# Seven block products in place of eight in the down projection of a decoder layer

## The chip, the cores and the metric

The kernel runs on one core of one Trainium2 chip. The metric is the device time of one execution in microseconds (us). A core has a matrix engine (PE; PEld is its loading of the stationary operand), a vector engine (DVE), an activation engine (ACT), a GpSimd engine (POOL) and a queue (SP) from which all loads and stores of this part are issued. Each engine works through its own instructions in order and waits where an operand is not there yet.

## The reference

One decoder layer on 512 tokens of width 1024: a token mixer with a residual, then a gated convolutional feed-forward part with a residual, then a final RMSNorm. The change touches the last matrix product of the feed-forward part, the residual beside it and the final norm:

```python
D_MODEL = 1024; SEQ = 512; FFN_DIM = 2816
def conv_ffn(h, w_up, conv_w, conv_b, w_down):
    up = h @ w_up
    ... # causal depthwise convolution of width 3, plus conv_b
    gate, val = jnp.split(up, 2, axis=-1)
    return (jax.nn.silu(gate) * val) @ w_down
...
    x = x + conv_ffn(h, w_up[l], conv_w[l], conv_b[l], w_down[l])
return rmsnorm(x, norm_final)
```

The down projection is thus a product of 512 tokens by 2816 (k) with 2816 by 1024 columns, in float32.

## The kernel before

Every float32 operand of a matrix product is split into a high part that the matrix engine takes whole (`whi`, `gh`, `hTh`) and the low rest (`wlo`, `gl`, `hTl`), and each product is three matmuls (`mm3`, `mm3m`): high by high, high by low, low by high. A matmul takes 128 of k and 128 stationary columns and streams 512 moving columns.

The order of all work is written out by hand. `units` is a list of pieces of PE work, each with the weight chunk that it needs; `run` goes through it, and for each unit it first has the chunks of the next ones loaded (SP), split (`Chunk.split`: ACT copies the high part, DVE subtracts it to get the low one), then emits what was put into `plan` with `before` or into `later`, and then the unit's matmuls. The list `early` says which chunks are split some units ahead. High and low pieces of weights have four buffers each (`whi`, `wlo`), so ACT may write a new one only when PE is through with the one that was there four pieces earlier.

The feed-forward part has two stages. In the up stage 11 steps of c each make 256 of the 2816 hidden values: four units of 24 matmuls (gate and value, two tiles of 128 each), whose results pass through the convolution (`conv`: one ACT instruction, two of DVE), silu and the product gate times value; the product is split into `gh` and `gl`, which stay in SBUF for all 22 tiles of k. In the down stage the tokens are the stationary operand and the weights move: for each half of 512 columns there are six chunks of up to four k tiles, and four accumulators in PSUM, one for each tile of 128 tokens (`down_unit`). After the first half the sum is added to the residual `x1` (which stays in SBUF), squared for the norm, and multiplied by the gain of the final norm. The last chunk of the second half goes token tile by token tile, so that the first three tiles are finished while PE works on the next; the last tile is done in two pieces of 256 columns. `finish` takes the reciprocal root on POOL, scales one half on ACT and the other on DVE, and stores them.

## Time and profile before

| what | value |
|---|---|
| median of 3 runs | 839.66 us (839.02 to 839.73) |
| profiled execution: time | 839.8 us |
| profiled execution: span from first to last instruction | 838.0 us |
| PE busy | 815.6 us (97% of the span) |
| DVE, ACT, POOL busy | 474.1, 354.5, 164.5 us |
| granted clock of TensorE, mean | 0.991 of full |

The span is what the trace covers; the time of an execution also has 1.8 us around it. A busy share is the time in which an engine had an instruction under way. The matmuls of PE overlap: one that lasts 0.39 us in the trace starts 0.227 us after the one ahead of it, so the pitch from start to start is the cost of one in a row of them.

### The profile page before, as it was taken

Reading aid. Unit: us, or ns where it says so; the run is one execution under the profiler, and the core shown is the slowest. Engines: PE = TensorE matmul, PEld = TensorE weight load, DVE = VectorE, ACT = ScalarE, POOL = GpSimd, SP = SyncE. Lnnn points to the kernel's source line nnn. Section 1 sums busy time; section 2 is a strip of 40 time slices with the busy share of each in tenths; the row PEclk is TensorE's granted clock in tenths of the full one; section 3 lists DMA queues with packets and bytes.
Section 4 is the critical chain, followed back from the end, with each engine's and each line's share of the span. In section 5 each row is a group of like instructions: output and inputs, shape, how many; then the busy total and the mean of one; then the engine's idle time right before and its main releaser. Section 6 shows DMA issues by size and latency. Waiting matters only on the chain.

```text
span 838.0 us, 10521 instructions
## 1 busy us (share of the span) xinstructions
PE 815.6 (97%) x4085; PEld 675.9 (81%) x4085; DVE 474.1 (57%) x921; ACT 354.5 (42%) x665; POOL 164.5 (20%) x217
## 2 busy tenths in 40 slices
PE   8999899997999999999999999999999999999996
PEld 7978768775787888888878998888888888888885
DVE  7998387484645637263655456555655555422313
ACT  6446455434435555352444344444444443313212
POOL 6199652441200100023520000000000000002002
PEclk9999989998999999999999999999999999999999
DMA  9332031121322113232261313333233323412402
GB/s 241 102 104 97 1 100 52 51 79 46 78 68 90 52 51 102 79 101 72 101 236 65 101 52 101 101 101 100 101 101 100 102 76 101 153 61 89 151 0 101
DMA packets 68277, 76.60 MB, mean 91 GB/s; under 512 B 8160, under 2 KB 55556, under 8 KB 68228
## 3 DMA queue, kind: packets, MB, share of 16 engines
q1 hardware_dynamic: 67972, 75.89, 28.2%
q8 instruction: 32, 0.52, 0.3%
q0 software_dynamic: 256, 0.05, 0.1%
q14 instruction: 17, 0.14, 0.1%
HBM read 73.81 MB, written 2.12 MB: 91 GB/s over the span
## 4 chain that ended last, share of the span: by engine, by line
PE 80%; POOL 8%; DVE 6%; ACT 2%; issue 2%; DMA 2%; SPq 0%; POOLq 0%; DVEq 0%; ACTq 0%
PE up L171 10%; PE up L172 10%; PE up L173 10%; PE mm L171 9%; PE mm L173 9%; PE mm L172 9%; PE acc L178 6%; PE acc L179 6%; PE acc L177 6%; POOL esc L279 1%; POOL vt L279 1%; POOL t L279 1%; PE sc L898 1%; DMA raw<-in_w_in_dram 1%; PE o L722 1%
## 5 line engine op out<-in xcount | busy, mean ns | idle before, releaser
L92 DVE TENSOR_TENSOR wlo<-raw,whi 128x1024 fp32r<-128x1024 f32 (+1 forms) x126 | 150.0, 1200 | 136.0 <-ACT whi L66 135.8
L66 ACT ACTIVATE whi<-raw 128x1024 fp32r<-128x1024 f32 (+1 forms) x126 | 127.3, 1023 | 58.3 <-PE acc L179 56.2
L171 PE MATMUL up<-hTh,whi 128*128 128x512 f32 (+1 forms) x384 | 142.7, 372 | 0.0
L172 PE MATMUL up<-hTl,whi 128*128 128x512 f32 (+1 forms) x384 | 142.6, 371 | 0.0
L173 PE MATMUL up<-hTh,wlo 128*128 128x512 f32 (+1 forms) x384 | 142.6, 371 | 0.0
L171 PE MATMUL mm<-hTh,whi 128*128 128x512 f32 (+1 forms) x336 | 133.9, 399 | 2.7 <-ACT whi L66 2.7
L173 PE MATMUL mm<-hTh,wlo 128*128 128x512 f32 (+1 forms) x336 | 131.3, 391 | 1.6 <-DVE wlo L92 1.6
L172 PE MATMUL mm<-hTl,whi 128*128 128x512 f32 (+1 forms) x336 | 130.9, 390 | 0.0
L275 DVE SCALAR_TENSOR_TENSOR cc<-up,cpar,cc 128x511 f32<-128x511 f32 x88 | 65.9, 749 | 97.3 <-ACT cc L1110 95.7
L173 PEld LDWEIGHTS up<-hTh,wlo 128*128 128x128 f32 x384 | 72.4, 188 | 12.6
L171 PEld LDWEIGHTS up<-hTh,whi 128*128 128x128 f32 x384 | 72.4, 188 | 12.5
L172 PEld LDWEIGHTS up<-hTl,whi 128*128 128x128 f32 x384 | 72.4, 188 | 12.4
L171 PEld LDWEIGHTS mm<-hTh,whi 128*128 128x128 f32 x336 | 64.3, 191 | 17.9 <-ACT whi L66 3.1
L173 PEld LDWEIGHTS mm<-hTh,wlo 128*128 128x128 f32 x336 | 64.2, 191 | 15.2 <-DVE wlo L92 2.0
L172 PEld LDWEIGHTS mm<-hTl,whi 128*128 128x128 f32 x336 | 64.2, 191 | 11.9
L177 PE MATMUL acc<-whi,gh 128*128 128x512 f32 x172 | 66.9, 389 | 0.0
L178 PE MATMUL acc<-wlo,gh 128*128 128x512 f32 x172 | 66.9, 389 | 0.0
L179 PE MATMUL acc<-whi,gl 128*128 128x512 f32 x172 | 66.9, 389 | 0.0
L279 POOL TENSOR_TENSOR x<-x,gfin 128x512 f32<-128x512 f32 x4 | 5.2, 1289 | 296.8 <-ACT acc L1049 296.8
L1110 ACT ACTIVATE cc<-up,cpar 128x512 f32<-128x512 f32 x44 | 34.3, 779 | 61.2 <-PE up L173 60.4
L992 ACT ACTIVATE th<-mm 128x512 f32<-128x512 f32 x24 | 14.3, 594 | 75.2 <-PE mm L173 75.2
L66 ACT ACTIVATE gh<-cc 128x512 fp32r<-128x512 f32 x22 | 13.9, 632 | 59.4 <-DVE cc L279 59.4
(298 smaller groups left out, 1266.1 us busy)
## 6 DMA issues: line engine op xcount, KB each, us to landing
raw<-in_w_up_dram SPq DMA_DIRECT2D x22, 1024.0 KB, 5.1
raw<-in_w_in_dram SPq DMA_DIRECT2D x18, 1024.0 KB, 5.1
raw<-in_w_down_dram SPq DMA_DIRECT2D x10, 1024.0 KB, 5.0
x<-in_x_dram SPq DMA_DIRECT2D x8, 512.0 KB, 6.6
raw<-in_w_in_dram SPq DMA_DIRECT2D x8, 512.0 KB, 5.3
raw<-in_w_out_dram SPq DMA_DIRECT2D x4, 1024.0 KB, 5.1
raw<-in_w_branch_a_dram SPq DMA_DIRECT2D x4, 512.0 KB, 6.0
raw<-in_w_branch_c_dram SPq DMA_DIRECT2D x2, 1024.0 KB, 5.0
```

What stands on the lines that cost most here:

```text
L66: S.activation(o, i, AF.Copy)
L92: (lo_eng or V).tensor_tensor(view(lo), r, view(hi).bitcast(F32), op=ALU.subtract)
L171: PE.matmul(ps, wh, xh, start=first, stop=False)
L172: PE.matmul(ps, wh, xl, start=False, stop=False)
L173: PE.matmul(ps, wl, xh, start=False, stop=last)
L177: PE.matmul(ps, xh, wh, start=first, stop=False)
L178: PE.matmul(ps, xh, wl, start=False, stop=False)
L179: PE.matmul(ps, xl, wh, start=False, stop=last)
L275: emit(lambda: V.scalar_tensor_tensor(o, a, s, b, op0=op0, op1=op1))
L279: emit(lambda: (eng or V).tensor_tensor(o, a, b, op=op))
L992: S.activation(t, ps, AF.Tanh, scale=0.5)
L1110: S.activation(dst, ps, AF.Identity, bias=cpar[:, 3, f:f + 1], scale=cpar[:, 2, f:f + 1])
```

## The change

The down projection is cut into halves of tokens, of k tiles and of columns, and these blocks are combined by a scheme of seven products (Strassen's, in Winograd's form): p1 to p7, each of 256 tokens by 1408 of k by 512 columns. Tokens and weights are first combined by sums and differences of blocks. For the weights, `Sum` loads one block at a time and, where `plus` names another, adds that one's raw block on DVE before the split: p5 is its own block plus that of p1, p6 adds p5's sum, p4 adds p6's sum, and p7 adds p3's block; p1, p2 and p3 use their block as it is. For the tokens, `sums` makes the combinations when a step of the up stage is done, and `late` splits the ones that have to wait for room.

The hidden values of each step c are the two halves of k (a = 0 and 1 of step c), so the scheme's k runs over 11 tiles, in groups of two (and one of one). There are two sweeps over k: the first accumulates p1, p5, p6 and p4 (eight banks of PSUM), the second p2, p7 and p3. Each pair of a group and a product is one unit: 12 matmuls, or 6 in the group of one (k0 = 10), which stands last in the first sweep and first in the second. `ends` puts the seven results together. The residual is written to DRAM in the up stage (`park`) and read back into the space of `hTh` when the up stage is over (`down_loads`); loads use six half-size buffers. The final norm is one instruction for each half row, after the last product.

```diff
+    class Sum:
+        def __init__(self, k0, nk, col, row):
+            self.k0, self.nk, self.col, self.row = k0, nk, col, row
...
+        def split(self, i, hi_eng=None, lo_eng=None):
+            r = self.raw
+            if self.plus is not None:
+                V.tensor_tensor(r, r, self.plus.raw, op=ADD)
+            hi, lo = (piece([128, 2, 512], n)[:, 0:self.nk, :] for n in ("whi", "wlo"))
+            copy_act(hi, r)
+            V.tensor_tensor(lo, r, hi.bitcast(F32), op=SUB)
+            self.p[0] = (hi, lo)
...
-                load_to(ci + 3)
+                load_to(ci + (6 if isinstance(c, Sum) else 3))
...
-            gh[f], gl[f] = slot([128, T], F32R, name="gh"), slot([128, T], F32R, name="gl")
-            copy_act(gh[f], v)
-            later.append(lambda: tt(gl[f], v, gh[f][:, :].bitcast(F32), SUB))
+            if a:
+                later.append(lambda: sums(c))
...
+    def sums(c):
...
+        v = cc[0][:, 2:4, :]
+        a11, a12, a21, a22 = (v[:, j, t * 256:t * 256 + 256] for t in range(2) for j in range(2))
+        s5 = s6 = a21
+        tt(R[c - c % 2, 4][:, Q1 if c % 2 else Q0], a11, a21, SUB)
+        tt(s5, a21, a22, SUB)
+        parts((c, 1), v[:, 0, :])
+        tt(s6, s5, a11, SUB)
+        two = lambda t: t.rearrange("p (j n) -> p j n", j=2)
+        if c < FULL:
+            parts((c, 2), v[:, :, Q1], two)
+        else:
+            R[c, 2] = store(F32)
+            copy_act(two(R[c, 2]), v[:, :, Q1])
+        R[c, 3] = store(F32)
+        copy_act(R[c, 3][:, Q0], a12)
+        tt(R[c, 3][:, Q1], a12, s6, ADD)
+
+    def late(c, i):
+        o = Q0 if (c, i) == (NP - 1, 4) else slice(0, T)
+        parts((c, i), R.pop((c, i))[:, o], lambda t: t[:, o])
...
+    def park():
+        for t in range(NT):
+            SY.dma_start(xd[t * 128:(t + 1) * 128, :], x1[t // 2][:, t % 2, :])
...
+    def down_loads():
+        SY.dma_start(x2[0], xd[:, :].rearrange("(t p) n -> p t n", p=128))
         SY.dma_start(gfin[0], norm_final[None, :].to_broadcast([128, DM]))
...
+    def down_unit(chunk, kind, k0, n, first, last):
         def fn():
...
+            for t in range(2):
+                if first:
+                    PS[kind, t] = bank(BANK[kind], name=kind)
+                for k in range(n):
+                    xh, xl = (v[:, t * 128:t * 128 + 128] for v in tok(k0 + k, kind))
+                    mm3m(PS[kind, t], xh, xl, chunk.get(k), first and k == 0,
+                         last and k == n - 1)
+                if last:
+                    ends(kind, t)
...
+    def ends(kind, t):
+        ps = PS[kind, t]
+        if kind == "p1":
+            es[t] = slot([128, 512], name="e")
+            copy_act(es[t], ps)
+            add_to(t, 0, ps)
+        elif kind == "p6":
+            tt(es[t], es[t], ps, ADD)
+        elif kind == "p4":
+            e, p5 = es[t], PS["p5", t]
+            add_to(2 + t, 0, e)
+            add_to(2 + t, 0, ps)
+            tt(e, p5, e, SUB)
+            later.append(lambda: (add_to(t, 1, e), add_to(2 + t, 1, e)))
+        elif kind == "p2":
+            add_to(t, 0, ps)
+            square(t, 0, ps)
+            part(t, 0)
+        elif kind == "p7":
+            add_to(2 + t, 0, ps)
+            add_to(2 + t, 1, ps, SUB)
+            square(2 + t, 0, ps)
+            square(2 + t, 1, ps)
+            part(2 + t, 0)
+            finish(2 + t)
+        elif kind == "p3":
+            add_to(t, 1, ps)
+            square(t, 1, ps)
+            finish(t)
...
     def finish(t):
+        ms = fss[:, 8 + t:9 + t]
+        part(t, 1)
         G.tensor_tensor(ms, ms, mhalf, op=ALU.pow)
...
+        for half in range(2):
+            o = slice(half * 512, half * 512 + 512)
+            stt(xv(t, half), xv(t, half), ms, gfin[0][:, o], MUL, MUL)
+            SY.dma_start(out[0, t * 128:(t + 1) * 128, o], xv(t, half))
...
+    SWEEPS = ((("p1", 0, 0, None), ("p5", 1, 0, "p1"), ("p6", 1, 1, "p5"), ("p4", 0, 1, "p6")),
+              (("p2", 0, 1, None), ("p7", 1, 0, "p3"), ("p3", 1, 1, None)))
+    GROUPS = [(c, min(2, NP - c)) for c in range(0, NP, 2)]
...
+    for i, (u, ch) in enumerate(sums_):
+        for d in (2, 3):
+            if i + d < len(sums_):
+                early.setdefault(u, []).append((sums_[i + d][1], 1))
...
+    before(u_up + 3, park)
+    before(u_down, down_begin)
+    before(u_down + 2, down_loads)
```

How the order of instructions moves is seen best on DVE, at three places. The first is the middle of the down stage. Before, DVE has only the subtractions that make the low parts of the weights:

```order
L92 TENSOR_TENSOR wlo_6023<-raw_5926,whi_6022 128x1024 [waits DMAHW1_49,Activation_49]
L92 TENSOR_TENSOR wlo_6027<-raw_5926,whi_6026 128x1024 [waits Activation_49]
L92 TENSOR_TENSOR wlo_6081<-raw_5969,whi_6080 128x1024 [waits DMAHW2_49,Activation_49]
L92 TENSOR_TENSOR wlo_6085<-raw_5969,whi_6084 128x1024 [waits Activation_49]
L92 TENSOR_TENSOR wlo_6139<-raw_6030,whi_6138 128x1024 [waits DMAHW4_49,Activation_49]
```

In the changed kernel this is one group of the first sweep (k0 = 4), from the split of p1 to that of p4; L187 is the sum of two raw blocks, L190 the subtraction for the low part, and `op` the low part of a late token combination:

```order
L190 TENSOR_TENSOR wlo_6098<-raw_5912,whi_6097 128x1024 [waits DMAHW2_49,Activation_49]
L308 TENSOR_TENSOR op_6103<-op_5283,op_6102 128x512 [waits Activation_49]
L187 TENSOR_TENSOR raw_5912<-raw_5912 128x1024 [waits DMAHW3_49]
L190 TENSOR_TENSOR wlo_6120<-raw_5912,whi_6119 128x1024 [waits Activation_49]
L187 TENSOR_TENSOR big_5989<-big_5989,raw_5912 128x1024 [waits DMAHW4_49]
L190 TENSOR_TENSOR wlo_6138<-big_5989,whi_6137 128x1024 [waits Activation_49]
L187 TENSOR_TENSOR big_5989<-big_5989 128x1024 [waits DMAHW7_49]
L190 TENSOR_TENSOR wlo_6156<-big_5989,whi_6155 128x1024 [waits Activation_49]
```

Three sums have come in, and each stands right ahead of the subtraction of the same block, which waits for ACT (the high part of that sum).

The second place is where the first sweep ends and the second begins; before, the nearest thing is the end of the first half of columns:

```order
L92 TENSOR_TENSOR wlo_6197<-raw_6088,whi_6196 128x1024 [waits DMAHW5_49,Activation_49]
L279 TENSOR_TENSOR x10_3896<-x10_3896,acc_5933 128x512 [waits PE_49]
L275 SCALAR_TENSOR_TENSOR fss_152<-fss_152,epsv_78 128x1 [waits Activation_49]
L279 TENSOR_TENSOR x10_3896<-x10_3896,acc_5934 128x512 [waits PE_49]
L275 SCALAR_TENSOR_TENSOR fss_152<-fss_152,epsv_78 128x1 [waits Activation_49]
```

In the changed kernel `x2` is the residual, `e` a copy of p1's result, and p4 to p6 are accumulators; the rows run from the subtraction for p3 (k0 = 10) to the sum for p7 of the next group (k0 = 0):

```order
L190 TENSOR_TENSOR wlo_6439<-raw_5912,whi_6438 128x512 [waits Activation_49]
L308 TENSOR_TENSOR x2_5988<-x2_5988,e_6396 128x512 [waits DVE_49]
L308 TENSOR_TENSOR x2_5988<-x2_5988,p4_6065 128x512 [waits DVE_49,PE_49]
L308 TENSOR_TENSOR e_6396<-p5_6023,e_6396 128x512
L308 TENSOR_TENSOR x2_5988<-x2_5988,e_6402 128x512
L308 TENSOR_TENSOR x2_5988<-x2_5988,p4_6072 128x512 [waits DVE_49,PE_49]
L308 TENSOR_TENSOR e_6402<-p5_6030,e_6402 128x512
L190 TENSOR_TENSOR wlo_6456<-raw_5912,whi_6455 128x1024 [waits DMAHW7_49,Activation_49]
L308 TENSOR_TENSOR x2_5988<-x2_5988,e_6396 128x512 x2
L308 TENSOR_TENSOR x2_5988<-x2_5988,e_6402 128x512 [waits DVE_49]
L308 TENSOR_TENSOR x2_5988<-x2_5988,e_6402 128x512
L187 TENSOR_TENSOR big_5989<-big_5989 128x1024 [waits DMAHW1_49,DMAHW0_49]
```

The additions that combine the products stand between the splits of the next weights.

The third place is the end of the program. Before:

```order
L275 SCALAR_TENSOR_TENSOR fss_152<-fss_152 128x1 [waits Activation_49]
L279 TENSOR_TENSOR x11_3897<-x11_3897,fin_6533 128x256 [waits PE_49]
L279 TENSOR_TENSOR cc_4381<-x11_3897,gfin_5971 128x256 [waits DVE_49]
L279 TENSOR_TENSOR x11_3897<-x11_3897,fin_6534 128x256 [waits PE_49]
L269 TENSOR_SCALAR cc_4381<-cc_4381,fss_152 128x512 [waits Pool_49]
L279 TENSOR_TENSOR cc_4381<-x11_3897,gfin_5971 128x256 [waits DVE_49]
L275 SCALAR_TENSOR_TENSOR fss_152<-fss_152 128x1 [waits Activation_49]
L275 SCALAR_TENSOR_TENSOR fss_152<-fss_152 128x1 [waits DVE_49,Activation_49]
L269 TENSOR_SCALAR cc_4381<-cc_4381,fss_152 128x512 [waits Pool_49]
```

In the changed kernel, from the second addition of p7's second token tile on:

```order
L308 TENSOR_TENSOR x2_5988<-x2_5988,p7_6486 128x512
L304 SCALAR_TENSOR_TENSOR fss_152<-fss_152,epsv_78 128x1 [waits Activation_49]
L304 SCALAR_TENSOR_TENSOR fss_152<-fss_152 128x1 [waits DVE_49,Activation_49]
L304 SCALAR_TENSOR_TENSOR x2_5988<-x2_5988,fss_152,big_5989 128x512 [waits Pool_49]
L304 SCALAR_TENSOR_TENSOR x2_5988<-x2_5988,fss_152,big_5989 128x512
L308 TENSOR_TENSOR x2_5988<-x2_5988,p3_6503 128x512 [waits PE_49]
L304 SCALAR_TENSOR_TENSOR fss_152<-fss_152 128x1 [waits Activation_49]
L304 SCALAR_TENSOR_TENSOR x2_5988<-x2_5988,fss_152,big_5989 128x512 [waits Pool_49]
L304 SCALAR_TENSOR_TENSOR x2_5988<-x2_5988,fss_152,big_5989 128x512 [waits DVE_49]
L308 TENSOR_TENSOR x2_5988<-x2_5988,p3_6507 128x512 [waits PE_49]
L304 SCALAR_TENSOR_TENSOR fss_152<-fss_152 128x1 [waits Activation_49]
L304 SCALAR_TENSOR_TENSOR x2_5988<-x2_5988,fss_152,big_5989 128x512 [waits Pool_49]
```

For each token tile DVE now goes through the whole chain from the addition over ACT and POOL to the scaling before it takes the next one.

## Rows read from the trace of the kernel before

**Rows 1.** The page's busy times (share of the span) and instructions by engine.
```profile
PE 815.6 (97%) x4085; PEld 675.9 (81%) x4085; DVE 474.1 (57%) x921; ACT 354.5 (42%) x665; POOL 164.5 (20%) x217
```

**Rows 2.** Busy time by engine of the up and down stages; columns in the first line.
```profile
core 0: us, PE busy (x) PEld busy (x) DVE busy (x) ACT busy (x) POOL busy (x), PEclk, DMA share, GB/s
475.00:711.00 236.00, 236.00 (x1117) 198.65 (x1116) 139.11 (x177) 102.09 (x135) 0.00 (x0) 1.00 0.30 96
711.00:831.00 120.00, 120.00 (x542) 99.80 (x540) 38.57 (x46) 29.88 (x42) 9.56 (x9) 1.00 0.25 86
```

**Rows 3.** Timeline of PE, first and last matmul of the down stage: start, duration.
```profile
711.13 0.39 PE L177 MATMUL acc<-whi,gh 128*128 128x512 f32 x1
...
830.85 0.28 PE L179 MATMUL fin<-whi,gl 128*128 128x256 f32 x1
```

**Rows 4.** Groups of the down stage, 711 to 838 us: busy, mean ns of one | idle before.
```profile
L177 PE MATMUL acc<-whi,gh 128*128 128x512 f32 x172 | 66.9, 389 | 0.0
...
L92 DVE TENSOR_TENSOR wlo<-raw,whi 128x1024 fp32r<-128x1024 f32 x21 | 25.6, 1235 | 54.9 <-ACT whi L66 54.9
...
L279 DVE TENSOR_TENSOR x<-x,acc 128x512 f32<-128x512 f32 x8 | 5.5, 687 | 20.8 <-PE acc L179 20.8
...
L269 DVE TENSOR_SCALAR cc<-cc,fss 128x512 f32<-128x512 f32 x4 | 1.9, 481 | 0.7 <-POOL fss L1214 0.7
```

**Rows 5.** Timelines of DVE and ACT: start, duration, idle before.
```profile
604.80 1.22 DVE L92 TENSOR_TENSOR wlo<-raw,whi 128x1024 fp32r<-128x1024 f32 x1
605.93 0.68 DVE L279 TENSOR_TENSOR gl<-cc,gh 128x512 fp32r<-128x512 f32 x1
606.53 0.69 DVE L279 TENSOR_TENSOR cc<-cc 128x512 f32<-128x512 f32 x1
...
712.15 1.54 DVE L275 SCALAR_TENSOR_TENSOR cc<-up,cpar,cc 128x511 f32<-128x511 f32 x2 [3.18 <-ACT cc L1110]
...
738.53 1.06 ACT L66 ACTIVATE whi<-raw 128x1024 fp32r<-128x1024 f32 x1 [4.38 <-PE acc L179]
...
739.63 1.23 DVE L92 TENSOR_TENSOR wlo<-raw,whi 128x1024 fp32r<-128x1024 f32 x1 [4.21 <-ACT whi L66]
```

**Rows 6.** DMA issues of 560 to 838 us: count, KB each, median us to landing.
```profile
raw<-in_w_down_dram SPq DMA_DIRECT2D x10, 1024.0 KB, 5.0
raw<-in_w_down_dram SPq DMA_DIRECT2D x2, 512.0 KB, 3.3
```

**Rows 7.** Timeline of PE after a long idle stretch in the mixer.
```profile
201.81 1.11 PE L737 MATMUL pt<-ident,pj 128*128 128x128 f32 x4 [5.36 <-ACT pj L66]
...
206.56 0.63 PE L171 MATMUL mm<-hTh,whi 128*128 128x512 f32 x1
206.99 0.63 PE L172 MATMUL mm<-hTl,whi 128*128 128x512 f32 x1
...
207.83 0.40 PE L171 MATMUL mm<-hTh,whi 128*128 128x512 f32 x1
```

**Rows 8.** Busy time and granted clock (PEclk) of two stretches of the mixer, columns as in rows 2.
```profile
56.00:60.00 4.00, 2.99 (x25) 2.62 (x25) 3.96 (x6) 3.86 (x8) 4.00 (x7) 1.00 0.40 136
201.00:207.00 6.00, 5.19 (x15) 4.22 (x16) 4.61 (x12) 2.28 (x4) 0.00 (x0) 0.50 0.00 0
```

**Rows 9.** Timelines of the norm's steps: one token tile at mid-stage, and the last ones.
```profile
771.17 0.69 DVE L279 TENSOR_TENSOR x<-x,acc 128x512 f32<-128x512 f32 x1 [1.08 <-PE acc L179]
...
771.90 0.60 ACT L1049 ACTIVATE acc<-x 128x512 f32<-128x512 f32 x1 [2.00 <-DVE x L279]
...
772.65 0.16 DVE L275 SCALAR_TENSOR_TENSOR fss<-fss,epsv 128x1 f32<-128x1 f32 x1 [0.79 <-ACT acc L1049]
...
832.73 0.55 POOL L1214 TENSOR_TENSOR fss<-fss,mhalf 128x1 f32<-128x1 f32 x1 [2.05 <-DVE fss L275]
...
833.31 0.72 ACT L68 ACTIVATE x<-x,fss 128x512 f32<-128x512 f32 x1 [1.18 <-POOL fss L1214]
...
834.49 0.38 SPq L1222 DMA_DIRECT2D out_dram<-cc  x1
```

More of the change, by code (lines that the diff above doesn't have):

```diff
@@ L167, in krows, with block, load, get @@
         return c
+    class Sum:
+        def __init__(self, k0, nk, col, row):
+            self.k0, self.nk, self.col, self.row = k0, nk, col, row
+            self.src = w_down[0].rearrange("(k h p) n -> p k h n", h=2, p=128)
+            self.defs, self.p, self.own, self.plus = [1], {}, False, None
+        def block(self, col, row):
+            return self.src[:, self.k0:self.k0 + self.nk, row, col * 512:col * 512 + 512]
+        def load(self):
+            self.raw = raw_tile(self.nk)
+            SY.dma_start(self.raw, self.block(self.col, self.row))
+        def split(self, i, hi_eng=None, lo_eng=None):
[6 more added lines that the diff above has]
+            self.p[0] = (hi, lo)
+        def get(self, k):
+            return tuple(t[:, k, :] for t in self.p[0])
     def mm3(ps, w, xh, xl, first, last):
@@ L212, in load_to @@
             while state["loaded"] < min(n, len(order)):
+                if isinstance(order[state["loaded"]], Sum) and rn[0] >= 4 and not RB:
+                    return
                 order[state["loaded"]].load()
@@ L1112, in conv @@
         stt(dst[:, 2:T], ps[:, 0:T - 2], cpar[:, 0, f:f + 1], dst[:, 2:T], MUL, ADD)
-    gh, gl, cc = {}, {}, []
+    cc = []
     fps = {}
@@ L1210, in hybrid_block, with down_begin @@
-    parts, rest = [], []
+    gfin, x2, RS, RB, RW, rn = [], [], [], [], [], [0]
+    xd = dr.tile([T, DM], F32, tag="xd", bufs=1, name="xd")
+    def park():
+        for t in range(NT):
+            SY.dma_start(xd[t * 128:(t + 1) * 128, :], x1[t // 2][:, t % 2, :])
+    def down_begin():
+        x2.append(hp_.tile([128, NT, DM], F32, tag="hTh", name="x2"))
+        big = hp_.tile([128, 4, DM], F32, tag="hTl", name="big")
+        gfin.append(big[:, 0, :])
+        RS.append(big[:, 1, 0:512])
+        RB.extend(big[:, j, :] for j in (2, 3))
@@ L1212, in finish, with part @@
+    es = {}
+    def part(t, half):
+        ms, ss = fss[:, 8 + t:9 + t], fss[:, 2 * t + half:2 * t + half + 1]
+        stt(ms, ss, 1.0 / DM, epsv if half == 0 else ms, MUL, ADD)
     def finish(t):
-        ms, row, y = fss[:, 8 + t:9 + t], x1[t // 2][:, t % 2, 0:512], cc[0][:, t, :]
+        ms = fss[:, 8 + t:9 + t]
+        part(t, 1)
         G.tensor_tensor(ms, ms, mhalf, op=ALU.pow)
-        def first():
-            copy_act(row, row, scale=ms)
-            SY.dma_start(out[0, t * 128:(t + 1) * 128, 0:512], row)
@@ L1337, in hybrid_block @@
     u_down = len(units)
-    for half in range(2):
-        k0 = 0
-        for n in (2, 4, 4, 4, 4, 4):
-            ch = krows(w_down[0], k0, n, half * 512)
-            add(ch, down_unit(ch, half, k0, n))
-            k0 += n
+    SWEEPS = ((("p1", 0, 0, None), ("p5", 1, 0, "p1"), ("p6", 1, 1, "p5"), ("p4", 0, 1, "p6")),
+              (("p2", 0, 1, None), ("p7", 1, 0, "p3"), ("p3", 1, 1, None)))
+    GROUPS = [(c, min(2, NP - c)) for c in range(0, NP, 2)]
+    sums_ = []
+    for i, sweep in enumerate(SWEEPS):
+        gs = GROUPS if i == 0 else GROUPS[-1:] + GROUPS[:-1]
+        for j, (k0, n) in enumerate(gs):
+            group = {kind: Sum(k0, n, col, row) for kind, col, row, _ in sweep}
+            for kind, col, row, plus in sweep:
+                ch = group[kind]
+                ch.plus = group.get(plus)
+                u = add(ch, down_unit(ch, kind, k0, n, j == 0, j == len(gs) - 1))
+                sums_.append((u, ch))
+                if kind == sweep[1][0]:
+                    nxt = gs[j + 1] if j + 1 < len(gs) else (NP - 1, 1) if i == 0 else None
+                    if nxt and (i == 1 or j + 1 == len(gs)):
+                        fs = [(c, 3) for c in range(nxt[0], nxt[0] + nxt[1])] + [(nxt[0], 4)]
+                    else:
+                        fs = [(c, 2) for c in range(nxt[0], nxt[0] + nxt[1]) if c >= FULL] if nxt else []
+                    for d, (c, o) in enumerate(fs):
+                        before(u + min(d, len(sweep) - 2), lambda c=c, o=o: late(c, o))
+    for i, (u, ch) in enumerate(sums_):
+        for d in (2, 3):
+            if i + d < len(sums_):
+                early.setdefault(u, []).append((sums_[i + d][1], 1))
+    early.setdefault(u_down - 1, []).append((sums_[1][1], 1))
     def st_(g):
@@ L1389, in hybrid_block @@
     before(u_up + 2, lambda: norm2(1, ("pt", "sc", "pt", "sc")))
-    before(u_down + 1, load_gfin)
+    before(u_up + 3, park)
+    before(u_down, down_begin)
+    before(u_down + 2, down_loads)
     run(cu[1], 2)
```

107 lines of the change are left out of this document (42 added, 65 removed).

## The prediction

> **What bounds the kernel now.** I read the busy times first: PE is busy for 97% of the span, DVE for 57%, ACT for 42% [rows 1]. By stretches, the up and the down stage both have PE busy all the time at full clock (1.00), and in the down stage DVE works 38.6 us of 120 and ACT 29.9 [rows 2]. The groups say what DVE waits for there: 21 subtractions of 1.235 us, 54.9 us of idle time ahead of them, ended by ACT, which itself runs in step with PE; PE's own idle time is 0.0 [rows 4]. So down there time is the number of matmuls times their pitch. The first starts at 711.13, the last at 830.85 [rows 3]; there are 516 of 512 columns (172 on each of three lines [rows 4]) and 24 of half that, 528 whole ones, so the pitch is 119.7 / 527.5 = 0.227 us. The profiled execution took 839.8 us for a span of 838.0, 0.14 us above the median of the runs; I sum against 839.8 and round.
>
> **What is removed.** Seven products of 2 token tiles, 11 k tiles and 3 matmuls are 462 matmuls in place of 528: 66 x 0.227 = 15.0 us less, if PE stays without gaps. A unit of 12 is 2.72 us, one of 6 is 1.36. The up stage's matmuls are unchanged.
>
> **The first sweep: sums on DVE.** The order shows sum, subtraction, sum, subtraction on DVE, and ACT's copy has to fall between the two of a pair. DVE takes its instructions in order, so it stands still during that copy. The sum itself is not in the trace; the nearest row is the subtraction of the same shape with two inputs, 1.23 us, and I take that for it. The handovers: ACT's copy of 1024 starts at 738.53 and lasts 1.06, the subtraction starts at 739.63 [rows 5], 0.04 us later; from DVE to ACT 771.17 + 0.69 to 771.90, again 0.04 [rows 9]. Where nothing is waited for, DVE starts the next instruction 1.13 us after one of 1024 columns (604.80 to 605.93) and 0.60 after one of 512 [rows 5]. One block with a sum thus costs DVE 1.23 + 0.04 + 1.06 + 0.04 + 1.13 = 3.50 us, against 2.72 for the unit on PE that uses it. A group of four (one without a sum, whose copy ACT makes while DVE subtracts p4's low part) is 1.13 + 3 x 3.50 = 11.6, and 0.6 more for each late token combination (one to two in a group), 12.2 to 12.8, against 10.9 on PE. Splits run up to three units ahead, but that lead is gone at once: the last convolution's two instructions end at 712.15 + 1.54 = 713.7 [rows 5], and then come two blocks with a sum (7.0), a product (0.6), p1's subtraction (1.1) and the five short sums and one copy of the last up step (about 3.1, an estimate from the 512-column rows). So the second group's first sum starts at about 725.4. From there DVE needs 12.2 + 12.8 + 12.8 + 11.7 (the next p1 is of half size) and, in the group of one, 3 x 2.0: the first sweep's splits end at 780.9. PE follows within a unit, at about 782; without gaps it would be there at 711.1 + 264 x 0.227 = 771.0. **Loss 11 us.**
>
> **Between the sweeps.** PE has only 6 matmuls for each product in the last unit group of the first sweep and the first of the second, while DVE has fourteen additions of 512 columns (0.69 each [rows 4], 0.60 in a row) to combine p1, p4, p5 and p6 besides the splits, and the second place in the order shows them ahead of what PE needs next. Walked along the order from 780.9: two additions 1.3, p2's low part 0.6, a late one 0.6, p7's sum, copy and low part 2.0, a late one 0.35, two additions 1.2, p3's low part 0.6, six additions, some behind each other, 3.8, the next p2 1.1, four additions 2.5, p7's block with its sum 3.5, a late one 0.6, p3's 1.1, a late one 0.7. That is 20.0 us, to 800.9; only then can PE take the sixth of the 12 matmuls of p2 (k0 = 0). Left are 7 of these and 14 units: 1.6 + 38.1, so PE ends at 840.5, where without gaps it would end at 711.1 + 462 x 0.227 = 816.0. **Loss 24.5 in both sweeps, 13.5 of it here.** In the rest of the second sweep only one of three blocks has a sum: 3.50 + 2 x 1.13 + 3 x 0.60 = 7.6 us of DVE against 8.2 on PE, so PE is the bound again and nothing is caught up beyond that.
>
> **The clock.** On the same walk PE has nothing to do from about 791 (p3 of the small group is through) to 798 (ACT has copied the token combination that p2 of k0 = 0 begins with). After 5.36 us of idle time in the mixer, matmuls came 0.43 us apart (206.56, 206.99) until 207.83, some 6 us after the restart at 201.81 [rows 7], at a granted clock of 0.50, that is 1.2 GHz [rows 8]. Ten matmuls at 0.43 in place of 0.227 cost 2.0 us. I add it: PE ends at 842.5.
>
> **The tail.** Before, PE ends at 831.1 and the span 6.9 us later. The third place in the order shows DVE going through four chains one behind the other. Their steps: addition 0.69, square with its read of the sum 0.75 (771.90 to 772.65), a short DVE step 0.2 [rows 9], POOL 0.55 and its handovers 0.1, two scalings of about 0.75 (the convolution's pair took 1.54 [rows 5]): 3.9 us for a tile of p3, 4.5 for one of p7 (two additions, two squares). p2's two tiles end on DVE 3.4 us ahead of PE's end, then two of p7 and two of p3 take 9.0 + 7.8 = 16.8, so DVE ends 13.3 us after PE; the last store is issued then and took 3.5 us to the end of the span (834.49 to 838.0) [rows 9]. Tail 16.8 in place of 6.9. **Loss 9.9 us.**
>
> **What costs nothing.** Up stage: five short sums in place of two subtractions, and copies of the same columns, 1.4 us more of DVE in each 21.8 us of PE; DVE is busy 139 us of 236 there [rows 2]. Parking writes 2 MB and reads 2 MB; at 1 MB in 5.0 us [rows 6] that is 10 us of a queue that is busy 30% [rows 2], and the reading, with the norm's gain 12.5 us, stands ahead of a weight block that is wanted some 15 us later. If it came at half that rate, 8 us would show: the upper bound. Weight blocks of 512 KB land in 3.3 us [rows 6] and have five units' time. A sum could at the least cost what the one-input instruction of 512 columns does, 0.48 [rows 4], twice that for 1024: 0.27 less for each of 18 sums, 5 us in all, the lower bound.
>
> **Sum.** -15.0 + 11.0 + 13.5 + 2.0 + 9.9 = +21.4: 839.7 + 21.4 = 861 us, **slower by 2.5%**.
>
> **Rivals.**
> (a) DVE is hidden. Busy time alone speaks for it: a group of the first sweep has 7 instructions of 1.13 and up to two of 0.60, 9.1 us against 10.9 on PE, and before the change DVE is idle two thirds of the stage. If the splits' lead of three units held, sweeps and turn would be lossless, and only the tail would count: 839.7 - 15.0 + 9.9 = 834.6, faster. It decides at the point where a block with a sum costs DVE less than 2.72 us. The idle time ended by ACT [rows 4] speaks against it, since the wait is now inside DVE's own row. The Trainium skill (Perfetto Trace Analysis, Identifying the Most-Contended Engine) has occupancy as a fair measure for Vector of how near it is to its limit; by that rule DVE would have room, and the time would be this one. Chance 0.08.
> (b) The gaps slow the clock. In the first sweep PE would stand 0.8 us in every 3.5. At 0.43 us a group is 48 x 0.43 = 20.6 us, 8.2 more than 12.4; over half the sweep's five groups that is 20 us: 881. Against it: a stretch with PE busy 2.99 of 4.00 us kept a clock of 1.00 [rows 8]. The Trainium skill (TensorE: Matmul & The Clock Gate, A second HAM failure mode: psum-queue depth-cycling) tells of a kernel whose frequent short idle times between groups of matmuls made the clock swing between its two levels; by that the time would be this one, and this trace, at 75%, does not show it. Chance 0.06.
> (c) The sweeps run as in (a) but the turn between them costs its 13.5: 848. For it: the turn's additions are needed whatever the splits' lead. Chance 0.06.
>
> **Chances and range.** 0.80 for the forecast, whose own range by the bounds above is 855 to 869. With (c) and a part of (b) taken in, 848 to 870. A measurement of this kernel can tell about 0.2% from no change. Faster by more than that: (a), 0.08. Within it: 0.02, a mixture of (a) and (c). Slower: 0.90.
>
> **What would show it.** Right: DVE rows of L187 and L190 with about 1.1 us of idle time ahead of each L190, ended by ACT; PE idle ended by ACT and DVE in the first sweep, its units 3.5 us apart; a PE gap of 6 us or so at the turn, followed by matmuls of 0.63 us; no PE gaps from the second sweep's third group on; four chains after PE's end and a tail of 16 to 17 us; PE's down stage some 131 us long. Wrong: L187 well under 1 us; PE without gaps in the first sweep; L190 waiting for a DMA (the reading of the parked residual); a low clock through the first sweep.

## Result and the profile after

The changed kernel takes 860.32 us (median of 4 runs, 860.15 to 861.61), the kernel before 839.69 in the same session: ratio 1.0251, 95% interval 1.0233 to 1.0268, slower. The forecast was 861.0, range 848 to 870. The profiled execution took 860.35 us for a span of 858.6. The page's busy times, which answer to [rows 1]:

```profile
PE 809.7 (94%) x4007; PEld 662.7 (77%) x4007; DVE 557.5 (65%) x1038; ACT 383.3 (45%) x715; POOL 156.6 (18%) x211
```

No engine is near full but PE, and PE has less to do than before (815.6). So the page alone doesn't say why the kernel is slower. The windows of the up stage, the first sweep, the turn and the rest do, columns as in [rows 2]:

```profile
core 0: us, PE busy (x) PEld busy (x) DVE busy (x) ACT busy (x) POOL busy (x), PEclk, DMA share, GB/s
475.00:711.00 236.00, 236.00 (x1110) 198.35 (x1109) 154.69 (x214) 103.04 (x143) 0.00 (x0) 1.00 0.31 103
...
711.00:782.00 71.00, 64.04 (x259) 48.53 (x257) 51.09 (x56) 27.68 (x35) 0.00 (x0) 0.98 0.57 194
782.00:801.00 19.00, 10.07 (x26) 5.51 (x24) 16.81 (x25) 6.97 (x11) 0.00 (x0) 0.70 0.51 170
801.00:842.00 41.00, 40.87 (x175) 33.41 (x175) 30.05 (x38) 20.81 (x31) 0.55 (x1) 0.97 0.28 92
```

The up stage is lossless as before. In the first sweep PE stands still 7 us of 71, with DVE busy only 51 (72%); in the turn PE works 10 us of 19, and DVE 16.8; from 801 on PE is busy all the time until its last matmul ends at 841.87. Which waits these are, the groups of 711 to 859 us show (mean ns of one, idle time ahead, what ended it):

```profile
L204 PE MATMUL p<-whi,op 128*128 128x512 f32 x144 | 59.3, 412 | 10.2 <-ACT op L66 6.0 <-ACT whi L66 3.5 <-DVE x L308 0.7
L205 PE MATMUL p<-wlo,op 128*128 128x512 f32 x144 | 59.2, 411 | 5.4 <-DVE wlo L190 5.4
...
L190 DVE TENSOR_TENSOR wlo<-raw,whi 128x1024 fp32r<-128x1024 f32 (+1 forms) x26 | 29.0, 1121 | 17.8 <-ACT whi L66 17.7
...
L66 ACT ACTIVATE whi<-raw 128x1024 fp32r<-128x1024 f32 (+1 forms) x26 | 25.0, 974 | 39.0 <-DVE raw L187 32.5 <-PE p L206 3.2 <-ACT op L66 2.1
```

This is a ring of waits: DVE's low-part subtraction (L190) waits for ACT's copy, ACT's copy for DVE's sum (L187), the next sum stands behind that subtraction on DVE, and PE waits for both. In [rows 4] PE had no idle time, and DVE's waits were for an ACT that ran in step with PE. The timeline of DVE shows one turn of the ring, the last four additions of the turn with the sum that has to wait behind them, and the end of the program (start, duration, idle before):

```profile
740.04 1.22 DVE L187 TENSOR_TENSOR big<-big,raw 128x1024 f32<-128x1024 f32 x1
742.46 1.23 DVE L190 TENSOR_TENSOR wlo<-big,whi 128x1024 fp32r<-128x1024 f32 x1 [1.21 <-ACT whi L66]
743.61 1.22 DVE L187 TENSOR_TENSOR big<-big 128x1024 f32<-128x1024 f32 x1
...
792.41 2.49 DVE L308 TENSOR_TENSOR x<-x,e 128x512 f32<-128x512 f32 x4
794.82 1.22 DVE L187 TENSOR_TENSOR big<-big 128x1024 f32<-128x1024 f32 x1
...
846.00 0.16 DVE L304 SCALAR_TENSOR_TENSOR fss<-fss 128x1 f32<-128x1 f32 x1 [0.59 <-ACT p L1271]
846.83 1.42 DVE L304 SCALAR_TENSOR_TENSOR x<-x,fss,big 128x512 f32<-128x512 f32 x2 [0.66 <-POOL fss L1326]
848.16 0.68 DVE L308 TENSOR_TENSOR x<-x,p 128x512 f32<-128x512 f32 x1
849.62 0.16 DVE L304 SCALAR_TENSOR_TENSOR fss<-fss 128x1 f32<-128x1 f32 x1 [0.79 <-ACT p L1271]
```

A block with a sum costs DVE 743.61 - 740.04 = 3.57 us, for a unit that PE does in 2.72. At the end DVE adds p3's first tile only at 848.16, 6 us after PE's last matmul, because it first finishes p7's two tiles, and in each waits for ACT and for POOL. PE's timeline, with the first and the last matmul of the down stage, three gaps and some of the slow matmuls behind them, as in [rows 3, 7]:

```profile
709.66 0.39 PE L204 MATMUL p<-whi,op 128*128 128x512 f32 x1
...
726.47 0.51 PE L204 MATMUL p<-whi,op 128*128 128x512 f32 x1 [1.60 <-ACT whi L66]
727.73 0.58 PE L205 MATMUL p<-wlo,op 128*128 128x512 f32 x1 [0.76 <-DVE wlo L190]
728.11 0.63 PE L206 MATMUL p<-whi,op 128*128 128x512 f32 x1
...
782.11 0.50 PE L204 MATMUL p<-whi,op 128*128 128x512 f32 x1
...
786.33 0.77 PE L204 MATMUL p<-whi,op 128*128 128x512 f32 x1 [1.89 <-ACT whi L66]
...
797.78 0.79 PE L204 MATMUL p<-whi,op 128*128 128x512 f32 x1 [5.99 <-ACT op L66]
...
800.86 0.80 PE L206 MATMUL p<-whi,op 128*128 128x512 f32 x1
...
841.48 0.39 PE L206 MATMUL p<-whi,op 128*128 128x512 f32 x1
```

The matmul at 782.11 is the first of the second sweep: ahead of 797.78, where the first full group (k0 = 0) starts, lie the 18 of the small one. So the first sweep ends at 782.1, PE's work at 841.87, and the tail is 858.6 - 841.9 = 16.7 us.

### The profile page after: what moved, and what is told of

Read it like the earlier page. It is cut to its first block, busy times and chain, and to the rows that moved or that the text cites. A ratio compares the mean times of both kernels' runs of the same rounds, so it can differ in the third digit from the quotient of the medians.

```text
span 858.6 us, 10621 instructions
## 1 busy us (share of the span) xinstructions
PE 809.7 (94%) x4007; PEld 662.7 (77%) x4007; DVE 557.5 (65%) x1038; ACT 383.3 (45%) x715; POOL 156.6 (18%) x211
## 4 chain that ended last, share of the span: by engine, by line
PE 68%; DVE 13%; POOL 8%; ACT 5%; issue 3%; DMA 1%; SPq 0%; POOLq 0%; DVEq 0%; ACTq 0%
PE up L198 9%; PE up L199 9%; PE up L200 9%; PE mm L198 9%; PE mm L200 8%; PE mm L199 8%; DVE wlo L190 3%; ACT whi L66 3%; DVE raw L187 2%; PE p L206 2%; PE p L205 1%; PE p L204 1%; DMA x<-in_x_dram 1%; POOL esc L308 1%; POOL vt L308 1%
## 5 line engine op out<-in xcount | busy, mean ns | idle before, releaser
L92 DVE TENSOR_TENSOR wlo<-raw,whi 128x1024 fp32r<-128x1024 f32 (+1 forms) x104 | 123.1, 1193 | 80.6 <-ACT whi L66 80.4
L66 ACT ACTIVATE whi<-raw 128x1024 fp32r<-128x1024 f32 (+1 forms) x132 | 131.6, 1008 | 43.9 <-DVE raw L187 35.2
L198 PEld LDWEIGHTS up<-hTh,whi 128*128 128x128 f32 x384 | 72.3, 188 | 12.5
L1326 POOL TENSOR_TENSOR fss<-fss,mhalf 128x1 f32<-128x1 f32 x4 | 2.2, 547 | 381.2 <-DVE fss L304 381.2
L204 PE MATMUL p<-whi,op 128*128 128x512 f32 x146 | 60.1, 412 | 10.2 <-ACT op L66 6.0
L205 PE MATMUL p<-wlo,op 128*128 128x512 f32 x146 | 59.9, 411 | 5.4 <-DVE wlo L190 5.4
L206 PE MATMUL p<-whi,op 128*128 128x512 f32 x146 | 59.4, 407 | 0.3
L190 DVE TENSOR_TENSOR wlo<-raw,whi 128x1024 fp32r<-128x1024 f32 (+1 forms) x28 | 31.4, 1128 | 18.9 <-ACT whi L66 18.9
```

The source lines that it names most:

```text
L66: S.activation(o, i, AF.Copy)
L92: (lo_eng or V).tensor_tensor(view(lo), r, view(hi).bitcast(F32), op=ALU.subtract)
L190: V.tensor_tensor(lo, r, hi.bitcast(F32), op=SUB)
L198: PE.matmul(ps, wh, xh, start=first, stop=False)
L204: PE.matmul(ps, xh, wh, start=first, stop=False)
L205: PE.matmul(ps, xh, wl, start=False, stop=False)
```

## The experiments

Theory A is that of the prediction: three separate losses on DVE (the ring in the sweeps, the additions in the turn, the chains in the tail) outweigh 15 us fewer matmuls. The main rival is that DVE's amount of work sets the pace, whatever its order. The kernel before took 838.44 to 839.21 us in the sessions of these runs; each ratio is against its own session.

**The sums in another order.** DVE makes the next block's sum while ACT copies the present one:

```diff
+        def sum_up(self):
+            if self.plus is not None and not self.summed:
+                V.tensor_tensor(self.raw, self.raw, self.plus.raw, op=ADD)
+            self.summed = True
...
             r = self.raw
-            if self.plus is not None:
-                V.tensor_tensor(r, r, self.plus.raw, op=ADD)
+            self.sum_up()
...
             copy_act(hi, r)
+            if self.next is not None:
+                self.next.sum_up()
             V.tensor_tensor(lo, r, hi.bitcast(F32), op=SUB)
...
+        ch.next = sums_[i + 1][1] if i + 1 < len(sums_) else None
```

> The sum of the next block is issued on DVE between ACT's copy of the present block and its subtraction; DVE has the same instructions, in another order. Theory A (DVE stands still for ACT's copy between a sum and its subtraction): a block with a sum then costs DVE two instructions of 1.13 us, 2.3 us in place of 3.57, less than a unit on PE (2.72). The first sweep goes at PE's pace and ends 9 to 11 us earlier, at 771 to 773; turn and tail stay as they are: 849 to 852 us. The idle time of about 1.2 us ahead of each subtraction in the first sweep is gone. Rival B (the amount of DVE's work, or its weight blocks' arrival, sets the sweep, not the order): within 2 us of 860.

Measured: 845.01 us, ratio 1.0073 (1.0058 to 1.0088). DVE in the first sweep, and then PE's only gaps from 711 on, the first matmul of the second sweep and the last:

```profile
727.75 1.22 DVE L187 TENSOR_TENSOR raw<-raw 128x1024 f32<-128x1024 f32 x1
728.89 1.22 DVE L197 TENSOR_TENSOR wlo<-raw,whi 128x1024 fp32r<-128x1024 f32 x1
730.03 0.68 DVE L315 TENSOR_TENSOR op<-op 128x512 fp32r<-128x512 f32 x1
730.63 1.22 DVE L187 TENSOR_TENSOR big<-big,raw 128x1024 f32<-128x1024 f32 x1
```
```profile
724.32 0.50 PE L212 MATMUL p<-wlo,op 128*128 128x512 f32 x1 [0.76 <-DVE wlo L197]
...
770.47 0.39 PE L211 MATMUL p<-whi,op 128*128 128x512 f32 x1
...
773.99 0.47 PE L211 MATMUL p<-whi,op 128*128 128x512 f32 x1 [0.64 <-DVE x L315]
775.88 0.50 PE L211 MATMUL p<-whi,op 128*128 128x512 f32 x1 [0.97 <-DVE x L315]
779.31 0.80 PE L211 MATMUL p<-whi,op 128*128 128x512 f32 x1 [2.45 <-ACT op L66]
782.89 0.80 PE L213 MATMUL p<-whi,op 128*128 128x512 f32 x1 [2.37 <-DVE op L315]
...
825.92 0.39 PE L213 MATMUL p<-whi,op 128*128 128x512 f32 x1
```

The subtraction follows the sum without the wait of 1.2 us, and from one sum to the next it is 2.88 us with a late token combination between them. PE has one gap in the first sweep, and the second sweep's first matmul is that of 770.47 (18 lie between it and 779.31, where k0 = 0 starts): 11.6 us earlier than 782.11, a little more than expected. But the whole gain is 1.0251 - 1.0073 = 1.8%, 15 us: from there to the start of PE's last matmul it is 55.5 us in place of 59.4, so the turn, which the edit leaves alone but for the order of its sums, lost 3.9 us less too. So the time is below the 849 to 852 that theory A gave. Order counts, not amount; the estimate was right for the sweep and missed what the turn gets of it.

**No sums at all.** `split` without the two lines of the sum; the output is then no longer the layer's.

> The sums of weight blocks are left out altogether, so each product is formed with its own block alone; all else, the loads and the matmuls too, is as in the changed kernel. It takes 18 instructions of 1.22 us from DVE. Theory A: what counts is only that the block's cost on DVE falls below the 2.72 us of a unit; here it is copy, handovers and subtraction, about 2.3 us, so the time is that of the kernel with reordered sums, less 1 to 2 us for the sum that stands in the turn: 847 to 851 us. Rival B (amount of work): clearly faster than the reordered kernel, by up to the other 10 us, with that one near 860. If the arrival of weight blocks is the limit, both stay near 860.

Measured: 843.16 us, ratio 1.0057 (1.0040 to 1.0074), 1.3 to 1.9 us less than with reordered sums: that difference is as theory A has it, while the time is below its 847 to 851, as the reordered kernel was below its own range. The edit takes more from DVE than was expected, 24 sums in place of 18: 20 of 1024 columns and 4 of 512, those of both sweeps (1038 DVE instructions become 1014). The first sweep in the reordered kernel, and then in this one, shows how little the amount matters:

```profile
711.00:771.00 60.00, 59.24 (x262) 48.70 (x261) 52.32 (x60) 29.26 (x39) 0.00 (x0) 1.00 0.69 243
```
```profile
711.00:771.00 60.00, 60.00 (x266) 49.71 (x265) 37.45 (x46) 30.09 (x40) 0.00 (x0) 1.00 0.70 251
```

DVE is busy 52.3 us of 60 in the one and 37.5 in the other, and PE 59.2 and 60.0. In the changed kernel DVE was busy 51.1 of 71 and PE lost 7. The rival of the amount is refuted.

**The turn, with POOL.** In the turn between the sweeps, e is added to the residual on POOL, and the rest of the combination comes later (`TURN[0]` is the number of the second sweep's first unit):

```diff
-            add_to(2 + t, 0, e)
             add_to(2 + t, 0, ps)
-            tt(e, p5, e, SUB)
-            later.append(lambda: (add_to(t, 1, e), add_to(2 + t, 1, e)))
+            tt(xv(2 + t, 0), xv(2 + t, 0), e, ADD, G)
+
+            def combine():
+                tt(e, p5, e, SUB)
+                tt(xv(t, 1), xv(t, 1), e, ADD, G)
+                tt(xv(2 + t, 1), xv(2 + t, 1), e, ADD, G)
+
+            before(TURN[0] + 4 + t, combine)
```

> Only the turn between the sweeps is changed: the additions of e to the residual go to POOL, and the combination p5 - e with its two additions comes two unit groups later, when PE is the bound. DVE loses 8 of the 14 additions there, about 5 us. Theory A (these additions hold back the splits that PE waits for): PE's idle stretch of 5.99 us shrinks to 1 to 2 us and little of the time at half clock is left, 5 to 7 us in all: 853 to 856 us. Rival C (POOL's additions are several times slower than DVE's 0.69 us and hold DVE or the accumulators up in their place, or another wait fills the stretch): 859 or more, PE's gap as long as before.

Measured: 860.47 us, ratio 1.0260 (1.0244 to 1.0275): no gain. PE, then DVE and POOL at the first of POOL's additions:

```profile
794.84 0.79 PE L204 MATMUL p<-whi,op 128*128 128x512 f32 x1 [3.50 <-ACT op L66]
...
808.79 0.50 PE L206 MATMUL p<-whi,op 128*128 128x512 f32 x1 [1.22 <-DVE op L308]
...
818.12 0.50 PE L206 MATMUL p<-whi,op 128*128 128x512 f32 x1 [0.78 <-DVE op L308]
```
```profile
788.92 1.98 DVE L190 TENSOR_TENSOR wlo<-raw,whi 128x1024 fp32r<-128x1024 f32 x1
790.82 2.28 DVE L187 TENSOR_TENSOR big<-big 128x1024 f32<-128x1024 f32 x1
...
788.53 3.48 POOL L308 TENSOR_TENSOR x<-x,e 128x512 f32<-128x512 f32 x2 [317.49 <-DVE x L308]
```

Theory A's 853 to 856 is missed, and so is rival C's gap "as long as before": the gap is 3.50 us for 5.99 and PE starts 2.9 us earlier (794.84 for 797.78), but two new gaps, 2.0 us together, come later in the sweep. While POOL adds, DVE's instructions of 1.22 us take 1.98 and 2.28: of POOL's 3.48 us 1.8 are lost to DVE.

**The turn, on DVE.** The additions of the changed kernel, two at a time in the second and third group, none on POOL:

```diff
-            add_to(2 + t, 0, e)
             add_to(2 + t, 0, ps)
-            tt(e, p5, e, SUB)
-            later.append(lambda: (add_to(t, 1, e), add_to(2 + t, 1, e)))
+            before(TURN[0] + 5 + 2 * t, lambda: (add_to(2 + t, 0, e), tt(e, p5, e, SUB)))
+            before(TURN[0] + 6 + 2 * t, lambda: (add_to(t, 1, e), add_to(2 + t, 1, e)))
```

> As the run with the turn alone, but POOL gets nothing: the eight additions (e to the residual, p5 - e, and its two additions, for two token tiles) stay on DVE and come two at a time in the second and third unit group of the second sweep; the sums stand as in the changed kernel. Theory A (DVE's additions hold the restart of PE back): PE starts again 4 to 5 us earlier than at 797.78, at 793 to 794; but a block with a sum still costs DVE 3.57 us there, which leaves some 0.6 us free in a group, so most of 8 x 0.6 = 4.8 us comes back as PE gaps later in the sweep: 856 to 859 us. Rival C (something else holds PE at the turn): the restart stays at 797 to 798, 860 us.

Measured: 861.88 us, ratio 1.0269 (1.0255 to 1.0283), above the 856 to 859 that theory A gave. PE:

```profile
793.42 0.50 PE L204 MATMUL p<-whi,op 128*128 128x512 f32 x1 [1.70 <-ACT op L66]
794.76 0.80 PE L206 MATMUL p<-whi,op 128*128 128x512 f32 x1 [0.61 <-DVE op L308]
...
817.80 0.56 PE L206 MATMUL p<-whi,op 128*128 128x512 f32 x1 [2.09 <-DVE op L308]
818.16 0.63 PE L204 MATMUL p<-whi,op 128*128 128x512 f32 x1
```

The restart does come 4.4 us earlier, so the additions hold it. All of it is lost again: DVE was busy 4.82 us of 5 in 817 to 822, PE waits 2.09 us at 817.80, and then there are slow matmuls a second time (0.63 us, granted clock 0.66 in 817 to 822). That second slow stretch was not in the estimate.

**Both.** The reordered sums and this turn together.

> The reordered sums and the turn of the run before together, tail as in the changed kernel. Theory A: with the reordered sums DVE has 2 us free in each group of the second sweep, so the eight additions are hidden there: 3 to 5 us less than the reordered sums alone (845.0), 840 to 842 us, PE's end at 821 to 823 in place of 826.3. Rival C (the late token combinations, not the additions, hold PE at the turn): within 1.5 us of 845.

Measured: 841.87 us, ratio 1.0037 (1.0022 to 1.0052), 3 us below the reordered sums alone, PE's last matmul at 822.65. The same edit that gained nothing beside the old order gains here: what it takes out of the turn must find room behind it, and the reordered sums make that room.

**The tail.** First form: the finishing of a tile comes behind the next tile's additions and squares, and the first half of p3's tiles is multiplied by the gain on POOL beforehand and scaled on ACT:

```diff
         elif kind == "p2":
...
+            if wait_:
+                finish(wait_.pop(0))
+            tt(xv(t, 0), xv(t, 0), gfin[0][:, 0:512], MUL, G)
         elif kind == "p7":
...
-            part(2 + t, 0)
-            finish(2 + t)
+            wait_.append(2 + t)
+            if t == 1:
+                finish(wait_.pop(0))
         elif kind == "p3":
...
-            finish(t)
+            wait_.append(t)
+            while len(wait_) > 1 - t:
+                finish(wait_.pop(0))
...
+            if half == 0 and t < 2:
+                copy_act(xv(t, half), xv(t, half), scale=ms)
+            else:
                 stt(xv(t, half), xv(t, half), ms, gfin[0][:, o], MUL, MUL)
```

> Only the tail is changed: the finishing of a token tile (root on POOL, scalings) stands behind the next tile's additions and squares on DVE, the first half rows of the tiles that p3 ends are multiplied by the gain on POOL beforehand and scaled on ACT, and partial sums of the norm are formed earlier. Theory A (four chains one behind the other on DVE): DVE no longer stands still for ACT and POOL within a chain, about 1.5 us in each, and loses two scalings; the tail falls from 16.7 to 9 to 11 us: 852 to 855 us, PE's end unchanged at about 842. Rival D (the tail is set by the transfers of the last stores or by the latency of the last tile's chain alone): less than 2 us gained, 858 or more.

Measured: 855.34 us, ratio 1.0203 (1.0188 to 1.0218), 4 us less than the changed kernel (by the ratios) and just above the 852 to 855 expected; PE's end is unchanged (841.5) and the tail 853.2 - 841.5 = 11.7, above the 9 to 11 expected. Rival D is out. Second form, alone: the last group in the order p7, p2, p3, and the norm in two steps (`root`: the sums and POOL's root; `scale`: the scalings and stores), with no products on POOL:

```diff
         elif kind == "p2":
...
+            if t == 0:
+                root(3)
+            scale(2 + t)
         elif kind == "p7":
...
-            part(2 + t, 0)
-            finish(2 + t)
+            if t == 1:
+                root(2)
         elif kind == "p3":
...
-            finish(t)
+            if t == 1:
+                root(0)
+                root(1)
+                scale(0)
+                scale(1)
...
-            for kind, col, row, plus in sweep:
+            final = i == 1 and j == len(gs) - 1
+            for kind, col, row, plus in (sweep[1], sweep[0], sweep[2]) if final else sweep:
```

> Only the tail, in this second form (order p7, p2, p3 in the last group, norm in two steps); sums and turn as in the changed kernel. Theory A (the tail is a loss of its own): PE's end stays at about 842, the tail falls from 16.7 to 8 to 9 us: 852 to 853 us. Rival: the tail can't fall alone, since DVE is late from the sweep: 857 or more.

Measured: 856.11 us, ratio 1.0206 (1.0190 to 1.0221); the tail is 854.2 - 843.5 = 10.7 us, 6 less, while PE ends 1.6 later (its down stage began 0.6 later, at 710.22, and the new order has one gap of 0.49). Theory A's 852 to 853 is missed by 3 us, of which 2 lie in the tail (8 to 9 expected) and 1.6 in PE's later end. Alone it is no better than the first form; the loss in the tail is one of its own, but a tail of 11 to 12 us remains in either.

**All three.** Reordered sums, the turn on DVE, the first form of the tail, and the order p7, p2, p3 in the last group:

> Reordered sums, the turn on DVE two groups later, the tail's finishing behind the next tile, and the last group of the second sweep in the order p7, p2, p3, so that p7's two chains lie under 24 matmuls of p2 and p3. Theory A (three places on DVE, each a loss of its own on top of 15 us fewer matmuls): PE ends at 821 to 823, the tail is one tile's chain and its stores, 7 to 9 us, 829 to 832 us: faster than the kernel before (838.4 on this chip) by about 1%. If the three places share one loss: above 838.

Measured: 840.11 us, ratio 1.0011 (1.0002 to 1.0020): not the 829 to 832 of theory A but above the 838 at which the three places were to share one loss. The trace puts the miss elsewhere: the tail is 838.7 - 825.8 = 12.9 us, so it is longer here than in its own run (11.7), and PE's end comes 2.7 us later than with sums and turn alone, of which 1.3 lie ahead of the down stage (its first matmul is at 711.07 for 709.76). DVE and POOL in the tail:

```profile
826.57 2.40 DVE L311 SCALAR_TENSOR_TENSOR x<-x,fss,big 128x512 f32<-128x512 f32 x2 [0.67 <-POOL fss L1340]
828.90 0.68 DVE L315 TENSOR_TENSOR x<-x,p 128x512 f32<-128x512 f32 x1
...
826.50 1.26 POOL L315 TENSOR_TENSOR x<-x,big 128x512 f32<-128x512 f32 x1
```

Beside POOL's product of 1.26 us two scalings take 2.40 us (1.42 at 846.83 in the changed kernel), and an addition stands behind them, on which the rest of the chain waits; that is 1 us of the miss, and the rest was not taken apart. So the last run takes the second form of the tail, and spreads the turn's additions over four groups (`TURN[0] + 4 + 5 * t` and `+ 7 + 5 * t`):

> The reordered sums, the additions of the turn on DVE spread over four unit groups, the last group in the order p7, p2, p3, and the final norm in two steps (root, then scalings one tile later on DVE), with nothing of the tail on POOL but the roots. Theory A: with POOL's multiplications gone DVE's pairs of scalings take 1.4 us again (2.40 beside POOL in the run before), and DVE no longer waits 0.66 to 0.79 us in each tile; the tail falls from 12.9 to 8 to 9 us and PE ends 1 to 2 us earlier: 833 to 836 us, below the kernel before. Rival: the tail is bound by something other than the waits and POOL: 839 to 841, tail 12 us or more.

Measured: 834.70 us (833.78 to 835.32), ratio 0.9949 (0.9936 to 0.9961), below the kernel before. PE, and the last DVE rows:

```profile
776.33 0.50 PE L211 MATMUL p<-whi,op 128*128 128x512 f32 x1 [1.72 <-ACT op L66]
...
813.89 0.50 PE L213 MATMUL p<-whi,op 128*128 128x512 f32 x1 [0.49 <-DVE op L315]
...
821.54 0.39 PE L213 MATMUL p<-whi,op 128*128 128x512 f32 x1
```
```profile
821.63 0.68 DVE L315 TENSOR_TENSOR x<-x,p 128x512 f32<-128x512 f32 x1
...
824.50 1.28 DVE L315 TENSOR_TENSOR x<-x,p 128x512 f32<-128x512 f32 x2
...
826.79 2.75 DVE L311 SCALAR_TENSOR_TENSOR x<-x,fss,big 128x512 f32<-128x512 f32 x4
```

PE ends at 821.9 in place of 841.9, the longest gap at the turn is 1.72 us in place of 5.99, and the tail is 832.7 - 821.9 = 10.8 us in place of 16.7. Together the edits at three places, all on DVE's order, get 25 us back, where the sums alone gave 15, the tail alone 4 to 5 and the turn alone nothing. The places are three, as theory A said, and one shared loss does not fit; but they are not independent, since the turn's edit pays only beside the reordered sums, and these take 3.9 us off the turn by themselves. This run changes the tail and the spread of the additions at once and does not part them. The tail misses the expected 8 to 9: DVE has p3's additions at 824.50 only, 2.6 us after PE's end, behind p2's second tile and the scalings of p7's second, and all eight additions and eight scalings of the four tiles fall to it after 815; it also still waits for ACT, 1.22 us at 819.97 and 0.79 at 823.10.

## Why the prediction was right

The forecast held to 0.7 us, and no step of it failed: the losses came at the three places that it named, by the waits that it named. That it held so closely is in part luck. The first sweep cost 1.5 us more than predicted and the low clock 0.9 us less, and the down stage began 1.5 us earlier than in the profile before, which no term of the sum foresaw.

- **What is removed** (15.0): the up stage is unchanged, the pitch at full clock is still that of before (rows of 0.39 us that start 0.22 to 0.23 apart), and from 804 on six matmuls take 1.36 us without a gap. No run takes out matmuls alone, but in the last run, which has all of the change's side work, the down stage keeps PE for 821.9 - 709.3 = 112.6 us, where before it was 120.0, which more than pays for a tail that is 3.9 us longer.
- **The first sweep: sums on DVE** (11): 3.57 us for a block with a sum, predicted 3.50; the sum itself 1.22, taken as 1.23; the second group's first sum at 724.03, predicted 725.4; the sweep's end on PE 782.1, predicted about 782. But the first down matmul came at 709.66, not 711.13, so the loss is 72.4 - 264 x 0.227 = 12.5 in place of 11, and the early start hid the difference. (The start moves from one profiled execution to the next: in the ten of the changed kernel and its variants it lies between 709.29 and 711.07.) Of the 12.5, PE's idle time is 7.0; the rest is low clock and the restarts, where the second matmul came 0.34 us after the first in place of 0.227. Not every unit was 3.5 us long, as foreseen: in the last two full groups two of four units took 3.5 to 3.9 us and two 2.7 to 2.9, 13.05 us together, where 12.2 to 12.8 was predicted. The run with the sums in another order takes 11.6 us of it back with no work removed: shown.
- **Between the sweeps and the clock** (13.5 + 2.0): from 782.11 to the end of the last pitch it took 59.6 us for 198 matmuls, 44.9 by the pitch: loss 14.7. The gap was 5.99 us, up to 797.78, ended by ACT's copy of a token combination, predicted from about 791 to 798; ten matmuls came 0.41 us apart or more behind it, at a granted clock of 0.50 (797 to 803), 1.2 GHz. The walk along DVE's order was exact: its sixth matmul of p2 was to start at 800.9 and started at 800.86, 18.75 us after 782.11 for 23 matmuls, 13.5 lost. But five of the ten slow matmuls lie ahead of that point, where PE waited for DVE anyway; from there to the end it took 40.85 us for 175 matmuls, 39.7 by the pitch, so the clock cost 1.1 us and not 2.0. For the same reason the fall behind the gap of 1.89 us (786.33, granted clock 0.51 in 786.3 to 789.5), which the prediction does not have, cost nothing. That the additions hold the restart is shown by the two runs that move them (restart 2.9 and 4.4 us earlier). That the loss would be the same whatever happens in the first sweep is not so: with the sums reordered it was 3.9 us less, and rival (c), which kept the whole price of the turn beside a sweep without loss, was too dear by that: its 848 against the 845.0 of the reordered sums.
- **The tail** (9.9): 16.7 for 16.8. On DVE p7's chains took 5.0 us each (4.5 predicted) and p3's 3.6 (3.9). Two forms that break the chains take 5 to 6 us off it: shown. What is left, 10.7 us, was not taken apart further.
- **What costs nothing**: DVE's extra 15.6 us in the up stage (154.7 for 139.1, 1.44 for each step of 21.8 us, predicted 1.4) left PE at 236 of 236, and no row of DVE, ACT or PE in the down stage has a DMA as its releaser, though the 512 KB blocks landed in 4.3 to 4.4 us for 3.3 in [rows 6].
- **Rivals.** (a) fails: DVE's order was the bound in the first sweep at 72% busy. The Trainium skill (Perfetto Trace Analysis, Identifying the Most-Contended Engine) takes occupancy as the measure for Vector; by that rule DVE had room and the time would have been 834.6; the trace disagrees. The Trainium skill's next advice (Perfetto Trace Analysis, Optimization Strategy), to look for the gaps on the engine and what ends them, is what finds the ring, and this trace agrees with it: 17.7 of the 17.8 us of idle time ahead of L190 end with ACT's copy. (b): a clock fall of this sort did occur in the first sweep, once, for nine matmuls from 727.73 on; DVE's sums went on 3.57 us apart beside it (727.59, 731.16), so it set no pace, and the 20 us of this rival did not come. In the five traces with the old order of sums the first sweep took the same 72.4 to 72.5 us.
- **The range.** The lower bound of 5 us on 861 gives 856, not the 855 that the prediction states; nothing hangs on it.

## What to carry to other kernels

When a change puts an operation in front of one that waits for another engine's answer to it, the cost is the whole round trip on the in-order engine, not the operation: compare that with the other engine's unit, and issue the next block's step inside the wait. Work that is moved out of a tight place has to be given room where it lands, or the gap only moves with it (two runs of the turn gained nothing alone, and 3 us once the sums had made room). An algorithm with fewer matmuls pays only what its side work leaves: here 15 us of matmuls less cost 20.6 us as first written and gained 0.5%, 4.3 us, with the side work in another order.
